# Down projections of the middle feed-forward groups in blocks of seven products

## The chip, the cores and the metric

The kernel runs on one core of a Trainium2 chip. Its time is the device time of one execution in microseconds. Five engines work beside each other and wait for one another by semaphores: TensorE (PE, matmuls; PEld is its loading of the stationary operand), VectorE (DVE), ScalarE (ACT), GpSimd (POOL) and SyncE (SP), which issues most transfers. Matmuls write to PSUM, which has eight banks of 128 x 512 fp32; all other tiles are in SBUF.

## What is computed

A model of two layers on 512 tokens of width 1024: each layer has a mixing part and a feed-forward part, each between two RMS norms and added to the residual `h`. The change concerns the feed-forward part alone:

```python
f = rmsnorm(h, ln_ffn_pre[layer])
f = (jax.nn.silu(f @ w_ffn_gate[layer]) * (f @ w_ffn_up[layer])) @ w_ffn_down[layer]
h = h + rmsnorm(f, ln_ffn_post[layer])
```

All is fp32. The inner width is 2816, which is 22 inner tiles of 128.

## The kernel before

**Three products for one.** To keep fp32 accuracy every operand is split into a high part, rounded to the matmul's type fp32r, and the low rest. `split` (line 239) makes both: ACT casts (`hi`), DVE subtracts (`lo`). `mm3` (lines 191 to 193) multiplies high by high, high by low and low by high, so each 128 x 128 block costs three matmuls. Weights are loaded by SP into `raw` tiles (128 x 1024, four buffers) and split into `whi`/`wlo` tiles (128 x 512, eight buffers each). Split activations lie in a pool of 36 tiles.

**The feed-forward part** (`feed_forward`, line 1150). The inner tiles 0 and 1 come first, apart from the rest; the others go in the groups of line 1154. For each group, gate and up are computed for two inner tiles at a time, then the group's hidden rows are multiplied by the down weights.

*Gate and up* (`Seven`, line 1018). For two inner tiles the product with `f` is a 2 x 2 block product (two inner tiles by two halves of 256 tokens each, and two halves of the width 1024) made with seven block products instead of eight, Strassen's way. One block product is 4 x 3 = 12 matmuls with the weights stationary and 256 tokens moving. `sums` makes the four sums of weights on DVE, `parts` splits a weight block, `run` makes one product, `carry` copies a PSUM tile with ACT so that later products can accumulate on it. The PSUM tiles are `x`, `p` and `q`. `end` makes the rows, by `gate_rows` (line 1169) or `up_rows` (line 1176): gate rows are scaled and passed through Silu, up rows are multiplied by them, which gives the hidden row `u` of one inner tile (128 x 512 tokens); line 1181 splits it into `fs`. The first pair of a layer runs as `FirstSeven`, with its gate and up products interleaved.

*Down* (lines 1231 to 1240). For each half `dh` of the output width, four PSUM tiles (one per block of 128 tokens, tags `mm` and `lg`) collect over all inner tiles of the group; here the hidden tokens are stationary and 512 output columns of the weights move. `down_weights` loads two inner tiles at a time (512 KB) and splits them. At the end DVE adds each PSUM tile to the running sum `ys[tb][dh]` in SBUF (line 1240).

The last group (18, 22) is handed to `tail_of` and is worked on with the norm that follows.

**Order.** The program is written down in one order, and a scheduler places each engine's instructions by that order as priority, taking a later one where an earlier one isn't ready in its own estimate. On the chip each engine then keeps its fixed order. A tile is taken from its pool when a buffer is free. `behind` and `high_priority` shift single pieces.

Of the kernel before, what the change touches and what calls it, by code (L numbers as in the profile page):

```python
# [15 lines left out]
P = 128  # L16
# [24 lines left out]
def hybrid(ctx: ExitStack, tc: tile.TileContext, i: dict, out: bass.AP):  # L41
# [26 lines left out]
    def temp(s, shape=(P, T), tag="t", bufs=4, dt=F32):  # L68
        return tp.tile(list(shape), dt, tag=tag, name=name(s), bufs=bufs)
# [4 lines left out]
    def ps(tag, shape=(P, T), s="ps"):  # L74
        return pp.tile(list(shape), F32, tag=tag, name=name(s), bufs=2 if tag == "tr" else 3)
# [55 lines left out]
    def pair_of_parts(n=512, aside=False):  # L131
        if aside:
            return act("whi"), act("wlo")
        return (wp.tile([P, max(n, 512)], F32R, tag="hi", name=name("whi"), bufs=8)[:, :n],
                wp.tile([P, max(n, 512)], F32R, tag="lo", name=name("wlo"), bufs=8)[:, :n])
# [44 lines left out]
    def down_weights(layer, k, dh, aside=False):  # L180
        return moving_pair(i["w_down"][layer, 4 * dh : 4 * dh + 4, :, k : k + 2, :]
                           .rearrange("m p k c -> p m (k c)"), aside)

    def token_products(o, x, w, tb, start, stop):

        c = slice(tb * P, (tb + 1) * P)
        return mm3(o.rearrange("p (m c) -> p m c", c=P), (x[0][:, c], x[1][:, c]), w, start, stop)
# [50 lines left out]
    def split(src, hi, lo, eng=None):  # L238
        last_parts[:] = A.copy(hi, src), (eng or V).tensor_sub(lo, src, hi)  # L239
# [22 lines left out]
    class Norm:  # L262


        def __init__(self, width=T):
            self.r4 = small("r4")
            self.acc, self.width = None, width
# [66 lines left out]
    def parts(s):  # L334
        return [(act(f"{s}hi"), act(f"{s}lo")) for _ in range(KT)]
# [682 lines left out]
    class Seven:  # L1018
# [28 lines left out]
        def product(self, o, w, n, more=False):  # L1047
            for k, w in enumerate(cut(w, P)):
                mm3(o, w, self.xs[n][k], k == 0 and not more, k == KT // 2 - 1, more)
# [100 lines left out]
    def feed_forward(layer, phase, xp, meanwhile=None):  # L1150

        nnorm = PairNorm()
        rb = rbc
        groups = ((2, 8), (8, 14), (14, 18), (18, 22))

        def hidden(gate, up, f, cols):
            c0, c1 = cols
            n = c1 - c0
            gr = temp("gr")
            V.tensor_mul(gr[:, :n], gate, rb[:, c0:c1])  # L1160
            s = temp("silu")
            A.activation(s[:, :n], gr[:, :n], AF.Silu)
            ff = temp("f")
            V.tensor_mul(ff[:, :n], up, s[:, :n])
            split(ff[:, :n], f[0][:, c0:c1], f[1][:, c0:c1])

        gates = [None] * 3

        def gate_rows(row, src, g):

            end = V.tensor_mul(g, src, rb)
            gates[2] = A.activation(g, g, AF.Silu, scale=-1.0 if row else 1.0)
            gates[row] = g
            return end

        def up_rows(row, src, u, fs):
            if row:
                end = V.scalar_tensor_tensor(out=u, in0=src, scalar=-1.0, in1=gates[1], op0=ALU.mult, op1=ALU.mult)
            else:
                end = V.tensor_mul(u, src, gates[0])  # L1180
            split(u, *fs[len(fs) - 2 + row])
            return end

        fs = [(act("fhi"), act("flo")) for _ in range(2)]

        def first(n, aside):
            return prepared(i["w_up" if n % 2 else "w_gate"][layer, n // 2], (KT, P), aside)

        def evac_first(outs, cols):
            for m in range(2):  # L1190
                hidden(outs[2 * m], outs[2 * m + 1], fs[m], cols)

        scaled = {}
        a, close = boundary(phase, G_MIX_POST + layer, G_FFN_PRE + layer, nnorm, rb, first, evac_first, scaled)
        w = [down_weights(layer, 0, dh) for dh in range(2)]
        close()
        xs, last = combined(a, scaled, xp)
        last()
        ys = [[plain("y") for _ in range(2)] for _ in range(TB)]
        for tb in range(TB):  # L1200
            for dh in range(2):
                o = ps("lg" if dh else "mm", s="y")
                for k in range(2):
                    token_products(o, fs[k], w[dh][k], tb, k == 0, k == 1)
                A.copy(ys[tb][dh], o)

        for gi, (k0, k1) in enumerate(groups):
            fs = []
            for m in range(k0, k1, 2):
                if meanwhile and m == k1 - 2 and gi == len(groups) - 1:  # L1210
                    next(meanwhile)
                fs += [(act("fhi"), act("flo")) for _ in range(2)]
                Kind = FirstSeven if m == 2 else Seven
                sevens((lambda: Kind(xs, lambda n: i["w_gate"][layer, m + n], gate_rows),
                        lambda: Kind(xs, lambda n: i["w_up"][layer, m + n],
                                     lambda row, src, t: up_rows(row, src, t, fs))), m == 2, m == k0)
            nk = k1 - k0
            if gi == len(groups) - 1:
                if layer:
                    with behind([gates[2]]):  # L1220
                        A.preload_act_table_set("natural_log_exp_and_others")
                if meanwhile:
                    next(meanwhile)

                eps = small("eps")
                V.tensor_mul(eps, nnorm.r4, nnorm.r4)
                V.reciprocal(eps, eps)
                V.tensor_scalar_mul(eps, eps, RMS_EPS)
                return tail_of(fs, lambda kp, dh, aside, k0=k0: down_weights(layer, k0 + 2 * kp, dh, aside), ys, eps,
                               layer == 1)  # L1230
            for dh in range(2):
                outs = [ps("mm" if tb < 2 else "lg", s="y") for tb in range(TB)]
                for kp in range(nk // 2):
                    w = down_weights(layer, k0 + 2 * kp, dh)
                    for x in range(2):
                        k = 2 * kp + x
                        for tb in range(TB):
                            token_products(outs[tb], fs[k], w[x], tb, k == 0, k == nk - 1)
                for tb in range(TB):
                    V.tensor_add(ys[tb][dh], outs[tb], ys[tb][dh])  # L1240


    def layer_b(phase, fp):
# [297 lines left out]
```

## Time and profile before

| | us |
|---|---|
| median of 3 runs | 1105.83 |
| lowest, highest | 1105.72, 1106.42 |
| the profiled execution | 1106.21 |
| its span, first to last instruction | 1104.1 |

The profile is of one execution. In its rows a line number is that of the helper that issued an instruction, so tiles tell parts apart: `x`, `a` (written as `p` above) and `e` (`q`) are PSUM tiles of gate and up, `y` those of down. Rows of the timeline give start, duration, engine, line, operation and tiles; in brackets stands the idle time ahead of an instruction and what ended it. A window row gives a stretch from start to end, its length, and the busy time and number of rows of each engine.

### The profile page before, as it was taken

To read this page: it belongs to the slowest core of one execution; us is meant where nothing else is said; L and a number is where in the kernel's file an instruction comes from. 1 tells how busy PE (TensorE), PEld (TensorE's weight loads), DVE (VectorE), ACT (ScalarE), POOL (GpSimd) and SP (SyncE) were. 2 spreads that over 40 slices of the span, in tenths; PEclk is the share of its full clock that TensorE was granted. 3 is DMA by queue.
4 is the path that set the end of the run, shared out by engine and by line. 5 is a ranking of instruction groups with operands and counts; after the bars stand their busy time and mean duration, and the time that the engine had idled before them with its cause. 6 is when DMAs were issued, how large, how long until landed. Compare 5 with 4: busy or idle time off the path is not lost.

```text
span 1104.1 us, 19424 instructions
## 1 busy us (share of the span) xinstructions
PE 1096.2 (99%) x7363; PEld 1001.4 (91%) x7363; DVE 870.0 (79%) x1714; ACT 683.5 (62%) x1428; POOL 24.3 (2%) x40
## 2 busy tenths in 40 slices
PE   9999999999999999999999999999999999999998
PEld 7998889999899899998988998889999899899996
DVE  7879759996697497796968789868996698587775
ACT  7776578664366264477747788878664266254464
POOL 0000000000000000001000000000000000000000
PEclk9999999999999999999999999999999999999999
DMA  7521331334134133255222554531234134233232
GB/s 268 161 80 54 119 115 39 115 115 134 58 115 138 58 111 115 77 157 171 74 79 63 156 133 121 145 115 39 77 111 138 58 114 132 61 110 120 77 96 77
DMA packets 64020, 118.64 MB, mean 107 GB/s; under 512 B 5236, under 2 KB 40072, under 8 KB 63928
## 3 DMA queue, kind: packets, MB, share of 16 engines
q1 hardware_dynamic: 63032, 116.57, 34.9%
q8 instruction: 58, 0.95, 0.4%
q0 software_dynamic: 192, 0.52, 0.2%
q10 hardware_dynamic: 704, 0.32, 0.1%
q14 instruction: 34, 0.28, 0.1%
HBM read 105.23 MB, written 2.10 MB: 97 GB/s over the span
## 4 chain that ended last, share of the span: by engine, by line
PE 94%; DVE 3%; ACT 2%; issue 1%; DMA 0%; SPq 0%; DVEq 0%; ACTq 0%
PE y L191 10%; PE y L193 10%; PE y L192 10%; PE a L192 5%; PE a L193 5%; PE a L191 5%; PE ps L191 4%; PE ps L193 4%; PE ps L192 4%; PE x L191 3%; PE x L192 3%; PE x L193 3%; PE e L191 3%; PE e L192 3%; PE e L193 3%; PE v L191 2%
## 5 line engine op out<-in xcount | busy, mean ns | idle before, releaser
L239 ACT CAST whi<-raw 128x512 fp32r<-128x512 f32 x460 | 278.2, 619 | 265.2 <-PE y L193 119.5
L239 DVE TENSOR_TENSOR wlo<-raw,whi 128x512 fp32r<-128x512 f32 x460 | 310.4, 688 | 128.6 <-ACT whi L239 125.2
L191 PE MATMUL y<-whi,fhi 128*128 128x512 f32 (+1 forms) x356 | 139.8, 393 | 0.0
L193 PE MATMUL y<-whi,flo 128*128 128x512 f32 (+1 forms) x356 | 139.2, 392 | 0.0
L192 PE MATMUL y<-wlo,fhi 128*128 128x512 f32 (+1 forms) x356 | 138.9, 390 | 0.0
L191 PE MATMUL x<-xshi,whi 128*128 128x256 f32 x320 | 90.1, 281 | 0.2
L191 PE MATMUL a<-xshi,whi 128*128 128x256 f32 x320 | 89.9, 281 | 0.0
L192 PE MATMUL a<-xslo,whi 128*128 128x256 f32 x320 | 89.8, 281 | 0.0
L192 PE MATMUL x<-xslo,whi 128*128 128x256 f32 x320 | 89.8, 281 | 0.0
L193 PE MATMUL a<-xshi,wlo 128*128 128x256 f32 x320 | 89.8, 280 | 0.0
L193 PE MATMUL x<-xshi,wlo 128*128 128x256 f32 x320 | 89.7, 280 | 0.0
L193 PEld LDWEIGHTS y<-whi,flo 128*128 128x128 f32 x356 | 66.8, 188 | 15.5 <-DVE flo L239 0.2
L192 PEld LDWEIGHTS y<-wlo,fhi 128*128 128x128 f32 x356 | 66.9, 188 | 15.0 <-DVE wlo L239 0.2
L191 PEld LDWEIGHTS y<-whi,fhi 128*128 128x128 f32 x356 | 66.9, 188 | 14.7 <-ACT fhi L239 0.3
L191 PE MATMUL ps<-xshi,whi 128*128 128x256 f32 (+1 forms) x224 | 68.4, 305 | 0.0
L192 PE MATMUL ps<-xslo,whi 128*128 128x256 f32 (+1 forms) x224 | 66.6, 298 | 0.0
L193 PE MATMUL ps<-xshi,wlo 128*128 128x256 f32 (+1 forms) x224 | 66.3, 297 | 0.0
L191 PEld LDWEIGHTS x<-xshi,whi 128*128 128x128 f32 x320 | 60.2, 188 | 0.6 <-ACT x L1055 0.6
L192 PEld LDWEIGHTS a<-xslo,whi 128*128 128x128 f32 x320 | 60.2, 188 | 0.3
L191 PEld LDWEIGHTS a<-xshi,whi 128*128 128x128 f32 x320 | 60.2, 188 | 0.3
L193 PEld LDWEIGHTS a<-xshi,wlo 128*128 128x128 f32 x320 | 60.3, 188 | 0.0
L193 PEld LDWEIGHTS x<-xshi,wlo 128*128 128x128 f32 x320 | 60.3, 188 | 0.0
(310 smaller groups left out, 3056.1 us busy)
## 6 DMA issues: line engine op xcount, KB each, us to landing
raw<-in_w_gate SPq DMA_DIRECT2D x44, 512.0 KB, 3.5
raw<-in_w_up SPq DMA_DIRECT2D x44, 512.0 KB, 3.5
raw<-in_w_down SPq DMA_DIRECT2D x44, 512.0 KB, 3.9
raw<-in_w_out SPq DMA_DIRECT2D x16, 512.0 KB, 3.7
raw<-in_w_b_q SPq DMA_DIRECT2D x8, 512.0 KB, 4.5
raw<-in_w_a_v SPq DMA_DIRECT2D x6, 512.0 KB, 7.8
raw<-in_w_a_u SPq DMA_DIRECT2D x6, 512.0 KB
raw<-in_w_v SPq DMA_DIRECT2D x6, 512.0 KB, 3.5
```

The costliest lines, as they stand in the source:

```text
L191: PE.matmul(o, w[0], x[0], start=start, stop=False, skip_group_check=more)
L192: PE.matmul(o, w[0], x[1], start=False, stop=False, skip_group_check=more)
L193: return PE.matmul(o, w[1], x[0], start=False, stop=stop, skip_group_check=more)
L239: last_parts[:] = A.copy(hi, src), (eng or V).tensor_sub(lo, src, hi)
```

## The change

The groups are now (2, 6), (6, 10), (10, 14), (14, 18) and (18, 22). For all but the last, the down product of two inner tiles is itself a 2 x 2 block product: two inner tiles, two halves of the tokens (256 each) and the two halves of the output width. It is made with seven products instead of eight.

`Inner` takes the two hidden rows `u0` and `u1` of a pair and makes the seven left operands: the left half of `u0` (`first`), `u1` whole (two operands), and two tiles of differences and sums (`both`, `other`, two operands each), all split. For the first pair of a group (`aside`) the low parts of the last two are made otherwise: ACT writes the negative of the high part, and a DMA issued by POOL adds the source to it. `DownSeven` loads both halves of a pair's down weights, makes four sums on DVE and splits seven blocks. `product` multiplies one of them with two blocks of 128 tokens, 6 matmuls of 512 columns. `down_sevens` runs the products of both pairs of a group, a and b, in an order that shares PSUM tiles between outputs; it holds eight. Of the outputs, some are copied to SBUF by ACT and added to one or two `ys` tiles by accumulating DMAs from POOL (`put`), others are added by DVE (`final`). Gate and up, `carry` among them, stay as they were.

```diff
-        groups = ((2, 8), (8, 14), (14, 18), (18, 22))
+        groups = ((2, 6), (6, 10), (10, 14), (14, 18), (18, 22))
...
-            split(u, *fs[len(fs) - 2 + row])
+            if done:
+                done(row, u)
+            else:
+                split(u, *fs[len(fs) - 2 + row])
...
+        def split_aside(src, hi, lo, aside):
+            if not aside:
+                return split(src, hi, lo)
+            A.copy(hi, src)
+            A.activation(lo, hi, AF.Copy, scale=-1.0)
+            G.dma_start(lo, src, accum_op=ALU.add)
...
+            def combine(self, u0, u1):
+                left, right = (slice(*c) for c in HALVES)
+                first = tp.tile([P, 2, 256], F32R, tag="acc", name=name("b11"), bufs=2)
+                split(u0[:, left], first[:, 0, :], first[:, 1, :])
+                second, both, other = [(act("fhi"), act("flo")) for _ in range(3)]
+                split(u1, *second)
+                V.tensor_sub(u0[:, left], u0[:, right], u0[:, left])
+                V.tensor_sub(u0[:, right], u1[:, right], u0[:, right])
+                V.tensor_sub(u1[:, right], u0[:, left], u1[:, right])
+                V.tensor_add(u1[:, left], u1[:, right], u1[:, left])
+                split_aside(u0, *both, self.aside)
+                split_aside(u1, *other, self.aside)
+                half = lambda pair, c: tuple(t[:, c] for t in pair)
+                self.x = {1: (first[:, 0, :], first[:, 1, :]), 2: half(second, left), 3: half(second, right),
+                          4: half(other, left), 5: half(both, left), 6: half(other, right), 7: half(both, right)}
...
+        class DownSeven:
...
+                a11, a12, a21, a22 = (r[:, :, x, :] for r in raws for x in range(2))
+                self.w = {4: a22}
+                s3 = temp("s3").rearrange("p (m c) -> p m c", m=4)
+                V.tensor_sub(s3, a11, a21)
+                self.w[1] = self.parts(a11)
+                V.tensor_add(a21, a21, a22)
+                self.w[2] = self.parts(a12)
+                V.tensor_sub(a11, a11, a21)
+                V.tensor_add(a12, a11, a12)
+                self.w.update({3: a12, 5: a21, 6: a11, 7: s3})
...
+            def product(self, outs, n, start, stop):
+                w = self.w[n]
+                if n > 2:
+                    w = self.parts(w)
+                for x, o in enumerate(outs):
+                    c = slice(x * P, (x + 1) * P)
+                    mm3(o, tuple(t[:, c] for t in self.x[n]), w, start, stop, True)
+
+        def down_sevens(pairs):
+
+            def put(x, *where):
+                some = prob("yo")
+                A.copy(some, x)
+                for tb, dh in where:
+                    G.dma_start(ys[tb][dh], some, accum_op=ALU.add)
+
+            def final(x, tb, dh):
+                V.tensor_add(ys[tb][dh], x, ys[tb][dh])
+
+            a, b = DownSeven(pairs[0]), None
+            chain = [ps("lg", s="yc") for _ in range(2)]
+            a.product(chain, 1, True, False)
+            lows = [ps("mm", s="yl") for _ in range(2)]
+            a.product(lows, 2, True, False)
+            shared = [ps(t, s="ys") for t in ("tr", "tr")]
+            a.product(shared, 7, True, False)
+            ups = [ps(t, s="yu") for t in ("mm", "lg")]
+            a.product(ups, 3, True, False)
+            b = DownSeven(pairs[1])
+            b.product(chain, 1, False, True)
+            for x in range(2):
+                put(chain[x], (x, 0))
+            b.product(shared, 7, False, True)
+            for x in range(2):
+                put(shared[x], (x, 1), (x + 2, 1))
+            for u in (a, b):
+                u.product(chain, 6, False, u is b)
+            for x in range(2):
+                A.copy(shared[x], chain[x])
+            b.product(ups, 3, False, True)
+            for x in range(2):
+                final(ups[x], x + 2, 0)
+            a.product(chain, 5, False, False)
+            a.product(shared, 4, False, False)
+            b.product(lows, 2, False, True)
+            for x in range(2):
+                final(lows[x], x, 0)
+            b.product(chain, 5, False, True)
+            for x in range(2):
+                put(chain[x], (x + 2, 0), (x + 2, 1))
+            b.product(shared, 4, False, True)
+            for x in range(2):
+                final(shared[x], x, 1)
...
+                if gi < len(groups) - 1:
+                    pairs.append(Inner(m, m < k1 - 2))
...
-            for dh in range(2):
-                outs = [ps("mm" if tb < 2 else "lg", s="y") for tb in range(TB)]
...
-                for tb in range(TB):
-                    V.tensor_add(ys[tb][dh], outs[tb], ys[tb][dh])
+            down_sevens(pairs)
```

More of the change, by code (lines that the diff above doesn't have):

```diff
@@ L1174, in gate_rows, with up_rows @@
             return end
-        def up_rows(row, src, u, fs):
+        def up_rows(row, src, u, fs, done):
             if row:
@@ new lines, in feed_forward, with __init__, __call__ @@
+        class Inner:
+            def __init__(self, k, aside):
+                self.k, self.aside, self.u = k, aside, {}
+            def __call__(self, row, u):
+                self.u[row] = u
+                if len(self.u) == 2:
+                    self.combine(self.u[0], self.u[1])
+            def combine(self, u0, u1):
[13 more added lines that the diff above has]
+                          4: half(other, left), 5: half(both, left), 6: half(other, right), 7: half(both, right)}
@@ new lines, in feed_forward, with __init__, parts @@
+        class DownSeven:
+            def __init__(self, pair):
+                self.x = pair.x
+                raws = []
+                for dh in range(2):
+                    raw = wp.tile([P, 1024], F32, tag="raw", name=name("raw"), bufs=4)
+                    last_load[0] = nc.sync.dma_start(
+                        raw.rearrange("p (m c) -> p m c", m=4),
+                        i["w_down"][layer, 4 * dh : 4 * dh + 4, :, pair.k : pair.k + 2, :].rearrange("m p k c -> p m (k c)"))
+                    raws.append(raw.rearrange("p (m k c) -> p m k c", m=4, k=2))
+                a11, a12, a21, a22 = (r[:, :, x, :] for r in raws for x in range(2))
[8 more added lines that the diff above has]
+                self.w.update({3: a12, 5: a21, 6: a11, 7: s3})
+            def parts(self, src):
+                pair = pair_of_parts()
+                split(src, *(t.rearrange("p (m c) -> p m c", m=4) for t in pair))
+                return pair
+            def product(self, outs, n, start, stop):
[5 more added lines that the diff above has]
+                    mm3(o, tuple(t[:, c] for t in self.x[n]), w, start, stop, True)
@@ L1207, in feed_forward @@
         for gi, (k0, k1) in enumerate(groups):
-            fs = []
+            fs, pairs = [], []
             for m in range(k0, k1, 2):
@@ L1211, in feed_forward @@
                     next(meanwhile)
-                fs += [(act("fhi"), act("flo")) for _ in range(2)]
+                if gi < len(groups) - 1:
+                    pairs.append(Inner(m, m < k1 - 2))
+                else:
+                    fs += [(act("fhi"), act("flo")) for _ in range(2)]
                 Kind = FirstSeven if m == 2 else Seven
@@ L1215, in feed_forward @@
                         lambda: Kind(xs, lambda n: i["w_up"][layer, m + n],
-                                     lambda row, src, t: up_rows(row, src, t, fs))), m == 2, m == k0)
+                                     lambda row, src, t: up_rows(row, src, t, fs, pairs and pairs[-1]))), m == 2, m == k0)
             nk = k1 - k0
@@ L1230, in feed_forward @@
                                layer == 1)
-            for dh in range(2):
-                outs = [ps("mm" if tb < 2 else "lg", s="y") for tb in range(TB)]
[L1233 to L1236, printed above, removed]
-                        for tb in range(TB):
-                            token_products(outs[tb], fs[k], w[x], tb, k == 0, k == nk - 1)
-                for tb in range(TB):
-                    V.tensor_add(ys[tb][dh], outs[tb], ys[tb][dh])
+            down_sevens(pairs)
     def layer_b(phase, fp):
```

## The prediction

> **What bounds the kernel now.** I read the page first, for the shares of the engines.
>
> ```profile
> span 1104.1 us, 19424 instructions
> ## 1 busy us (share of the span) xinstructions
> PE 1096.2 (99%) x7363; PEld 1001.4 (91%) x7363; DVE 870.0 (79%) x1714; ACT 683.5 (62%) x1428; POOL 24.3 (2%) x40
> ```
>
> PE is never without work, but a busy PE may be a slow PE, so I then cut the feed-forward stage into its alternating parts with the view that sums engines over windows. The windows are, for layer 0, gate and up of a group, its down block, and so on through the three groups that are changed; then those three groups as a whole for each layer; last, one stretch early in layer 1.
>
> ```profile
> core 0: us, PE busy (x) PEld busy (x) DVE busy (x) ACT busy (x) POOL busy (x), PEclk, DMA share, GB/s
> 202.22:262.33 60.11, 60.07 (x505) 59.85 (x504) 54.24 (x98) 39.97 (x82) 0.00 (x0) 1.00 0.41 124
> 262.33:295.74 33.41, 33.41 (x147) 27.03 (x145) 17.84 (x30) 8.61 (x14) 0.00 (x0) 1.00 0.26 79
> 295.74:355.34 59.60, 59.60 (x505) 59.60 (x504) 52.04 (x89) 38.12 (x76) 0.00 (x0) 1.00 0.39 116
> 355.34:388.75 33.41, 33.41 (x146) 27.05 (x145) 17.81 (x30) 8.61 (x14) 0.00 (x0) 1.00 0.25 78
> 388.75:428.53 39.78, 39.78 (x337) 39.77 (x336) 33.29 (x58) 24.99 (x50) 0.00 (x0) 1.00 0.41 121
> 428.53:450.80 22.27, 22.27 (x98) 18.03 (x97) 15.12 (x25) 6.11 (x10) 0.00 (x0) 1.00 0.22 69
> 202.22:450.80 248.58, 248.54 (x1729) 231.32 (x1728) 190.35 (x322) 126.42 (x246) 0.00 (x0) 1.00 0.35 105
> 784.12:1032.13 248.01, 247.89 (x1730) 230.66 (x1728) 190.14 (x322) 126.66 (x246) 0.00 (x0) 1.00 0.35 105
> 797.00:835.00 38.00, 37.88 (x320) 37.48 (x319) 37.97 (x69) 25.08 (x51) 0.00 (x0) 1.00 0.32 102
> ```
>
> The step from one matmul to the next is what counts, and the code gives their number: 504 matmuls of 256 columns in 59.60 us is 0.118 us each; 144 of 512 columns in 33.41 us is 0.232, and 96 in 22.27 us is 0.232 again. The steps are the same in every part and the clock is full, so there is no waiting in these stretches: **PE is the bound, by the number of its matmuls.** A removed 512-column matmul is worth 0.232 us.
>
> DVE is the second engine: 190.35 of 248.58 us (77%), unevenly: about 90% beside gate and up, 53% to 68% beside the down blocks. From 797 to 835 it is full (37.97 of 38.00). What it costs when it is pressed is read from starts that follow each other:
>
> ```profile
> 428.44 0.68 DVE L1178 SCALAR_TENSOR_TENSOR s<-s,s 128x512 f32<-128x512 f32 x1
> 429.04 0.68 DVE L1180 TENSOR_TENSOR s<-x,s 128x512 f32<-128x512 f32 x1
> 429.64 0.68 DVE L239 TENSOR_TENSOR wlo<-raw,whi 128x512 fp32r<-128x512 f32 x1
> ...
> 805.77 0.42 DVE L1117 TENSOR_TENSOR s<-e,s 128x256 f32<-128x256 f32 x1
> 806.11 0.42 DVE L1118 TENSOR_TENSOR s<-a,s 128x256 f32<-128x256 f32 x1
> ```
>
> Rows overlap: a 512-wide one takes 0.60 us of the engine, a 256-wide one 0.34.
>
> Last, what DVE and ACT wait for while PE is in a down block (timeline, then costliest groups by form).
>
> ```profile
> 428.62 0.62 ACT L239 CAST whi<-raw 128x512 fp32r<-128x512 f32 x1 [0.81 <-PE x L192]
> ...
> 434.30 0.62 ACT L239 CAST whi<-raw 128x512 fp32r<-128x512 f32 x1 [2.16 <-PE y L193]
> 437.08 0.62 ACT L239 CAST whi<-s 128x512 fp32r<-128x512 f32 x1 [2.16 <-PE y L193]
> ```
> ```profile
> L239 ACT CAST whi<-raw 128x512 fp32r<-128x512 f32 x460 | 278.2, 619 | 265.2 <-PE y L193 119.5 <-PE a L192 38.8 <-PE x L192 37.8
> ...
> L1240 DVE TENSOR_TENSOR y<-y,y 128x512 f32<-128x512 f32 x48 | 29.7, 682 | 0.0
> L1205 ACT COPY y<-y 128x512 f32<-128x512 f32 x16 | 9.4, 588 | 8.4 <-PE y L193 8.1
> ```
>
> Each cast of a weight half waits for PE to finish with an older one: all eight hi/lo buffers are full, so the preparation stands about seven products ahead of PE at the end of a gate/up part. That lead is what the change will draw on.
>
> **The change, part by part.**
>
> PE. Per pair of inner tiles the direct product takes 2 tiles x 4 token blocks x 2 halves x 3 = 48 matmuls; seven products over two token blocks take 7 x 2 x 3 = 42. Eight pairs a layer, two layers: 96 matmuls fewer, 96 x 0.232 = **22.3 us**. Gate and up keep their matmuls. The cut into four groups instead of three adds one passage per layer from up to down, which costs nothing in the rows above (no part is longer than its matmuls).
>
> DVE, per layer. Weights: 7 splits instead of 4 per pair and 4 sums, +7 rows x 8 pairs x 0.60 = 33.6 us. Hidden rows: a pair set aside (four a layer) has 0.34 + 0.60 + 4 x 0.34 = 2.30 in place of two splits at 1.20, +1.10; the other four also split two more tiles, 3.50, +2.30; together 13.6. Output: before, 24 additions a layer (half of the x48 of L1240), after 4 groups x 6 = 24, so nothing. Sum **+47.2 us**. All of it is hidden by PE as long as DVE fits: PE's new time per layer is 248.3 - 11.1 = 237.2. DVE's by busy time is 190.2 + 47.2 = 237.4 (100%); but busy counts 0.68 where the engine is free after 0.60, and by the steps the 322 rows, 32 of them 256 wide, are 290 x 0.60 + 32 x 0.34 = 184.9, with the change 232.1 (98%). So the cover is nearly used up: five microseconds a layer are left, and every wait of DVE beyond them is paid by PE.
>
> ACT, per layer: 24 weight casts x 0.62 = 14.9; hidden rows, four aside pairs with four more 512-wide copies at most, 4 x 2.3, and four others 4 x 1.0, some 13; eight PSUM copies a group x 0.59 = 18.9. In all +47 on 126.4, 173 of 237 (73%): it fits.
>
> POOL and DMA, per layer: ten accumulating transfers of 256 KB a group and two per aside pair, 48. The kernel before has no accumulating DMA; the nearest is the plain copy between partitions that POOL issues.
>
> ```profile
> raw<-in_w_down SPq DMA_DIRECT2D x44, 512.0 KB, 3.9
> ...
> memk<-memk POOLq DMA_DIRECT2D x4, 128.0 KB, 4.6
> ```
>
> A copy of 128 KB lands 4.6 us after its issue. For 256 KB with a read of the target I take 6 us, between 4.6 and twice that, 9.2. What waits for them is DVE's last additions: `lows` are added five products (7 us) after the chain's first copy is sent, and `shared` eight products (11 us) after its. So 6 us are hidden, and 9.2 would hold DVE back for some 2 us in a block, which the lead of seven products covers once.
>
> SP. The down weights are still 16 loads of 512 KB a layer, but a pair's two halves are needed together, and the first tile is released late (its last split, for product 4, is the twelfth of fourteen). By eight buffers and 1.39 us a product this split is done about 6.5 us into the block, the next gate's second load lands 3.9 us later, and the gate starts at 19.5: hidden.
>
> PSUM. The block holds all eight banks. The last two that it takes are the old up block's: `q`, free after the addition at L1083, and `x`, free after row 0's multiplication, 0.6 us after the last matmul; they are needed 2.8 and 4.2 us in. The copies of `chain` must end before product 6 writes on it, 1.4 us after: two copies of 0.59 just fit.
>
> The passage from up to down. From the last up matmul PE has four products of the older pair, 24 x 0.232 = 5.6 us, then product 1 and, at 7.0 us, product 7 of the younger pair. DVE needs by then 0.60 (row 0), 0.34 + 0.60 (b11, u1), 4 x 0.34 and 0.60: 3.5 us, and about 1 us of ACT copies between, 4.5 in all. That holds if both pairs' weight sums are made earlier, in the lead, as the rows at 428 show for the weights now. I take a stall of 0.5 us for six of the eight blocks.
>
> The first group of each layer is different, as DVE is full there. The chain of waits of layer 1 ends:
>
> ```profile
> 811.33 0.61 DVE raw L1044
> 811.95 0.02 issue
> 811.97 0.62 ACT whi L239
> 812.59 0.28 ACT x L1055
> 812.87 0.04 issue
> 812.91 0.38 PE x L191
> ```
>
> A DVE that is late holds ACT's cast, behind which ACT's PSUM copy is queued, for which PE waits. The aside pair's extra 1.10 us falls just ahead of this; I take 1.1 us there plus 0.4 for the first down block, 1.5 a layer.
>
> Sum: 22.3 - 6 x 0.5 - 2 x 1.5 = 16.3 us. The profiled execution took 1106.21 us with its span of 1104.1; 1106.2 - 16.3 = 1089.9, and as the median lies 0.4 us under that execution, **1089.5 us**. Without any stall it is 1083.5.
>
> **The rivals.** DVE becomes the bound. For: 98% by its steps, and outside full stretches it does wait for ACT. Against: from 797 to 835 it ran without a hole. Does it lose 5% to waits, its work is 232.1 x 1.05 = 243.7 a layer, 6.5 over PE's 237.2: the gain is 22.3 - 13.0 = 9.3, 1096.5 us. At 7% nothing is left.
>
> Slower: the passage from up to down is not prepared. If the younger pair's weights come behind the hidden rows on DVE, then from the last up matmul stand 4.1 us of hidden rows (both other splits with them), 3.6 of the older pair's sums and first splits, 1.2 for its products 7 and 3, 3.6 of the younger pair's and 0.6 for its product 7: 13.1 us against PE's 7.0. 6.1 us in each of eight blocks is 49 us, less 22.3: 1132 us. It decides from a stall of 22.3 / 8 = 2.8 us a block on. For: the hidden rows come first in the program, and raw tiles are four, all held by the two pairs. Against: the full buffers at 428, which show weights made before the hidden rows exist.
>
> The transfers come late. The Trainium skill, SBUF — State Buffer, section Who interferes with whom, has POOL unable to write the descriptors of its DMAs while VectorE is in a two-port mode, and says that tensor_tensor has no such mode. In this kernel's terms: DVE's addition of `lows` stands at the head of its queue until the transfer lands, and PE runs on for the seven prepared products, 10 us; it needs landings over 7 + 10 = 17 us. With 20 us each block would lose 3 us, 24 in all: 1107, no difference. The row of 4.6 us, issued while DVE was at work, does not point that way; I give it 0.02.
>
> No change in matmuls is not a rival: the count is in the code.
>
> **How the numbers follow.** About 0.2%, 2.2 us, is what a measurement of this kernel can tell. Forecast (1083 to 1095): 0.62. DVE bound in part (1095 to 1103.6): 0.14. Within 0.2%: 0.07, of it 0.05 by DVE at 7% and 0.02 by the transfers. Slower, by the passage or by DVE losing more: 0.17. Faster 0.76, same 0.07, slower 0.17. Eight in ten: from 1083, no stall at all, to 1104, nearly all of the DVE case.
>
> **What would show it.** Down blocks of 84 matmuls and 19.5 us with a step of 0.232 show the first term. DVE near 97% in the changed windows with PE steps of 0.118 beside gate and up show that the cover holds; PE gaps inside gate and up, with DVE full, show the DVE rival; a gap of PE ahead of the younger pair's products 1 or 7, released by DVE, shows the passage; DVE additions to `ys` that idle for a DMA show late transfers. I am wrong if the sum of gaps in the eight blocks is over 12 us, or if DVE's rows grow longer beside POOL's transfers.

## The result and the profile after

| | us |
|---|---|
| before, median of 4 runs | 1105.89 (1105.72 to 1106.42) |
| after, median of 4 runs | 1124.61 (1122.06 to 1125.12) |
| after / before | 1.0164, 95% interval 1.0146 to 1.0181 |
| predicted | 1089.5, range 1083 to 1104 |

The change makes the kernel 18.7 us slower; the prediction had it 16.3 us faster. The page of the kernel after first; of its queues (third part) the columns are packets, MB and the time of the packets as a share of 16 engines' span, of its transfers (last part) the size and the median time from issue to landing.

```profile
span 1123.4 us, 19912 instructions
## 1 busy us (share of the span) xinstructions
PE 1091.1 (97%) x7267; PEld 995.8 (89%) x7267; DVE 956.2 (85%) x1906; ACT 760.7 (68%) x1588; POOL 107.7 (10%) x136
...
q1 hardware_dynamic: 63032, 116.57, 33.6%
q0 software_dynamic: 14016, 25.70, 13.3%
...
y<-yo POOLq DMA_DIRECT2D x80, 256.0 KB, 8.1
```

PE has its 96 matmuls fewer (7363 before), yet its share fell from 99% to 97%: it now stands idle for some 32 us, against 8 before. DVE grew by 86.2 us and ACT by 77.2. Queue q0, which POOL issues, moved 0.52 MB before (0.2% of the sixteen DMA engines' time); now it moves 25.70 MB, nearly all of it accumulating transfers, and takes 13.3%: per MB 1.8 times what the loads of q1 take (13.3 / 25.70 against 33.6 / 116.57).

Where the time goes is read from the windows, cut as before: gate and up of a group, its down block, and so on. The columns are those of the same view in the prediction (busy time and rows of PE, PEld, DVE, ACT and POOL, granted clock, DMA share, GB/s). Layer 0 is the upper half to 498.28, layer 1 the rest.

```profile
203.64:244.02 40.38, 40.38 (x337) 40.03 (x336) 37.30 (x71) 27.90 (x60) 1.93 (x2) 1.00 0.42 118
244.02:264.15 20.13, 19.73 (x86) 15.66 (x85) 16.52 (x31) 11.78 (x23) 5.21 (x6) 1.00 0.57 138
264.15:307.71 43.56, 41.54 (x337) 41.36 (x336) 42.68 (x77) 29.02 (x59) 5.20 (x6) 0.96 0.59 155
307.71:327.22 19.51, 19.51 (x87) 15.79 (x85) 16.35 (x30) 11.10 (x21) 5.29 (x6) 1.00 0.61 156
327.22:370.78 43.56, 41.04 (x338) 40.11 (x336) 42.17 (x76) 29.34 (x60) 5.21 (x6) 1.00 0.61 149
...
390.25:435.06 44.81, 41.82 (x338) 41.44 (x337) 39.26 (x71) 26.82 (x54) 4.33 (x5) 0.96 0.55 137
...
454.55:498.28 43.73, 40.64 (x338) 40.05 (x336) 37.96 (x69) 27.62 (x58) 2.61 (x3) 1.00 0.56 153
791.78:832.00 40.22, 40.22 (x337) 40.02 (x336) 36.28 (x69) 27.84 (x59) 1.80 (x2) 1.00 0.42 119
832.00:853.32 21.32, 19.81 (x86) 15.68 (x85) 17.00 (x31) 11.40 (x22) 5.20 (x6) 1.00 0.53 123
853.32:896.42 43.10, 40.49 (x337) 39.89 (x336) 42.70 (x77) 29.41 (x60) 5.16 (x6) 1.00 0.61 160
...
915.94:959.49 43.55, 41.45 (x338) 41.27 (x337) 43.05 (x77) 29.91 (x60) 5.15 (x6) 0.96 0.62 151
...
978.96:1026.41 47.45, 43.28 (x337) 42.70 (x336) 39.54 (x71) 26.86 (x54) 4.27 (x5) 0.93 0.53 130
...
1045.87:1091.51 45.64, 42.04 (x337) 41.44 (x336) 33.91 (x58) 24.33 (x49) 2.58 (x3) 0.96 0.48 134
```

The down blocks (84 matmuls) are what was forecast: 19.5 us with PE busy throughout, and 20.13 and 21.32 for the first one of each layer. All the rest is lost *behind* a block: 336 matmuls at 0.1183 us are 39.75 us, and the eight gate/up parts that follow a block take 43.1 to 47.45, together 355.4 against 318.0, **37.4 us**. With 2.4 in the two first blocks (beyond 19.5) and 1.1 in the two first gate/up parts that is 41 us, against the 22.3 saved: 18.7 us slower. (In four of these parts DVE is busy for 97% or more of the window, 42.68 of 43.56 us in the first, which looks like the DVE rival of the prediction. The experiments say otherwise.)

What happens behind a block is seen best around 390. The same view in windows of 2 us, some left out:

```profile
384.00:386.00 2.00, 2.00 (x10) 1.66 (x9) 2.00 (x4) 0.74 (x2) 0.00 (x0) 1.00 1.13 208
...
392.00:394.00 2.00, 0.11 (x1) 0.14 (x2) 1.55 (x3) 0.71 (x2) 0.35 (x1) 1.00 1.08 254
...
396.00:398.00 2.00, 2.00 (x11) 2.00 (x10) 2.00 (x5) 0.62 (x2) 0.00 (x0) 0.50 1.13 229
...
400.00:402.00 2.00, 2.00 (x20) 2.00 (x19) 0.00 (x0) 1.20 (x3) 0.00 (x0) 1.00 0.22 64
```

From 380 to 398 all sixteen DMA engines are busy (nine windows with shares from 1.01 to 1.13). In this stretch lie POOL's transfers and, from SP's timeline, the next part's loads (start, duration of both issues, engine, line):

```profile
379.72 3.04 SPq L144 DMA_DIRECT2D raw<-in_w_up  x2
```

What waits for these loads is shown by DVE's timeline, then PE's.

```profile
392.45 0.69 DVE L1040 TENSOR_TENSOR s<-raw,raw 128x512 f32<-128x512 f32 x1 [2.11 <-DMA raw<-in_w_up]
393.06 1.28 DVE L1265 TENSOR_TENSOR y<-ys,y 128x512 f32<-128x512 f32 x2
```
```profile
391.57 0.28 PE L193 MATMUL a<-xshi,wlo 128*128 128x256 f32 x1
393.89 0.36 PE L191 MATMUL e<-t3hi,whi 128*128 128x256 f32 x1 [2.04 <-DVE y L1265]
...
395.03 0.41 PE L191 MATMUL e<-t3hi,whi 128*128 128x256 f32 x1
395.23 0.42 PE L192 MATMUL e<-t3lo,whi 128*128 128x256 f32 x1
```

The loads were issued by 382.76 and are used at 392.45, 9.7 us later. DVE stood idle for 2.1 us with the sum of weights of the next `Seven` (L1040, which needs both raw tiles) at the head of its queue. **Behind it stood the down block's last additions** (L1265, `y<-ys`), which free the PSUM bank into which PE's product writes `e`. So PE waited 2.04 us for an addition that stood behind a wait for a load. Then comes a second price: a microsecond after the gap the step of PE is 0.20 us (395.03 to 395.23) and no longer 0.118, and the granted clock of the window from 396 to 398 is 0.50. Over the whole profiled execution the mean granted clock fell from 0.999 to 0.989, an estimated 11 of the 1123 us at most.

The chain of waits in this stretch (start, duration, what) has a POOL transfer as its longest link, one into the `y` tile to which the addition adds. It landed at 392.56, just as the late load did, so here either alone would have held PE:

```profile
380.72 0.55 POOL y L1262
381.27 11.29 DMA y<-yo
...
393.06 0.70 DVE y L1265
...
393.89 0.36 PE e L191
```

This is one place. Over the whole run, the view of the line that issues these loads (L144) gives who waited for them (us, times) and their landing, after and, in the second fence, before; the third has PE's waits in the kernel after (waiter, what it waited for: us, times, longest).

```profile
  DVE s L1040: 36.2, 18
...
DMA to landing us min/median/max: 3.5/4.6/8.8
```
```profile
  DVE s L1040: 9.0, 8
...
DMA to landing us min/median/max: 3.4/3.5/5.1
```
```profile
PE a L191 <- ACT x L1055: 9.1, 4, 3.0
...
PE e L191 <- ACT whi L239: 6.7, 3, 2.6
...
PE e L191 <- DVE y L1265: 5.8, 5, 2.0
```

DVE's wait for weights in L1040 grew from 9.0 us to 36.2, and the median load lands in 4.6 us instead of 3.5. (The landing row doesn't hold every load: its largest is 8.8, and the one above took more.) PE then waits in three ways for what is queued behind L1040 on DVE: for DVE's additions; for ACT's cast (`whi`) of a later weight sum, which DVE makes behind L1040; or for ACT's PSUM copy (L1055), which stands behind a Silu (L1172) that waits for DVE's gate rows (L1171). Followed back in the chain view, the six longest of the waits of the second and third way (they end at 267.75, 857.48, 919.61, 471.12, 996.54 and 1062.92, 14.8 us together) come to an L1040 that had itself waited for its weights for 3.1 to 3.9 us.

### The profile page after: what moved, and what is told of

Read it like the earlier page. It is cut to its first block, busy times and chain, and to the rows that moved or that the text cites. A ratio compares the mean times of both kernels' runs of the same rounds, so it can differ in the third digit from the quotient of the medians.

```text
span 1123.4 us, 19912 instructions
## 1 busy us (share of the span) xinstructions
PE 1091.1 (97%) x7267; PEld 995.8 (89%) x7267; DVE 956.2 (85%) x1906; ACT 760.7 (68%) x1588; POOL 107.7 (10%) x136
## 3 DMA queue, kind: packets, MB, share of 16 engines
q1 hardware_dynamic: 63032, 116.57, 33.6%
q0 software_dynamic: 14016, 25.70, 13.3%
## 4 chain that ended last, share of the span: by engine, by line
PE 60%; DVE 18%; DMA 13%; issue 4%; ACT 4%; POOL 1%; DVEq 0%; SPq 0%; ACTq 0%
DVE wlo L239 6%; DMA raw<-in_w_gate 5%; PE y L191 4%; PE y L192 4%; PE y L193 4%; DMA y<-yo 4%; PE ps L191 4%; PE ps L193 4%; PE ps L192 4%; DMA raw<-in_w_down 3%; PE a L191 3%; PE a L193 2%; PE a L192 2%; PE v L191 2%; PE v L193 2%
## 5 line engine op out<-in xcount | busy, mean ns | idle before, releaser
L239 ACT CAST whi<-raw 128x512 fp32r<-128x512 f32 x492 | 293.1, 619 | 149.9 <-PE x L192 28.5
L239 DVE TENSOR_TENSOR wlo<-raw,whi 128x512 fp32r<-128x512 f32 x492 | 326.4, 684 | 30.9 <-ACT whi L239 29.3
L191 PE MATMUL a<-xshi,whi 128*128 128x256 f32 x320 | 90.8, 284 | 1.1 <-ACT e L1055 1.1
L191 PE MATMUL x<-xshi,whi 128*128 128x256 f32 x320 | 91.6, 286 | 0.3 <-ACT x L1055 0.3
L1262 POOL DMA_DIRECT2D y<-yo x80 | 69.6, 1263 | 210.9 <-ACT yo L1260 182.8
L191 PE MATMUL ps<-xshi,whi 128*128 128x256 f32 (+1 forms) x224 | 68.4, 305 | 0.0
L191 PEld LDWEIGHTS a<-xshi,whi 128*128 128x128 f32 x320 | 60.6, 189 | 2.6 <-ACT e L1055 2.2
L191 PEld LDWEIGHTS x<-xshi,whi 128*128 128x128 f32 x320 | 61.8, 193 | 1.0 <-ACT x L1055 0.9
L192 PEld LDWEIGHTS x<-xslo,whi 128*128 128x128 f32 x320 | 61.5, 192 | 0.0
L1040 DVE TENSOR_TENSOR s<-raw,raw 128x512 f32<-128x512 f32 x40 | 27.5, 688 | 36.4 <-DMA raw<-in_w_gate 32.4
L191 PE MATMUL e<-t3hi,whi 128*128 128x256 f32 x160 | 46.0, 287 | 12.5 <-ACT whi L239 6.7
L191 PE MATMUL a<-d2hi,whi 128*128 128x256 f32 x160 | 48.2, 302 | 9.1 <-ACT x L1055 9.1
L239 ACT CAST whi<-s 128x512 fp32r<-128x512 f32 x56 | 34.8, 621 | 31.1 <-DVE s L1040 16.2
```

Of the source, the lines that this page charges most:

```text
L191: PE.matmul(o, w[0], x[0], start=start, stop=False, skip_group_check=more)
L192: PE.matmul(o, w[0], x[1], start=False, stop=False, skip_group_check=more)
L1040: V.tensor_add(self.s3, a11, a21)
L1262: G.dma_start(ys[tb][dh], some, accum_op=ALU.add)
```

## The experiments

Three theories. **T1:** the accumulating transfers make the weight loads late. **T2:** DVE has too much work. **T3:** the order on DVE is at fault, a late load's consumer ahead of additions that could run. In the tables "wait" is DVE's at L1040 with its number, and the mean clock is the granted one, both of the profiled execution; ratios are to the kernel before on the same chip, with the 95% interval. Edits are to the kernel after unless said otherwise.

**Traffic and work, alone and together.** `e1_tiny_accum` keeps every instruction on every engine, but the accumulating transfers of the outputs move 16 of 128 partitions, so the other rows of those sums are left out. `e2_no_sums` leaves out the four sums of down weights, 64 DVE rows in all (1842 against 1906). `e9_tiny_no_sums` does both.

```diff
-                    G.dma_start(ys[tb][dh], some, accum_op=ALU.add)
+                    G.dma_start(ys[tb][dh][:16], some[:16], accum_op=ALU.add)
```
```diff
-                V.tensor_sub(s3, a11, a21)
...
-                V.tensor_add(a21, a21, a22)
...
-                V.tensor_sub(a11, a11, a21)
-                V.tensor_add(a12, a11, a12)
-                self.w.update({3: a12, 5: a21, 6: a11, 7: s3})
+                self.w.update({3: a12, 5: a21, 6: a11, 7: a21})
```

> The changed kernel, but each accumulating transfer into ys moves 16 of its 128 partitions (32 KB in place of 256 KB); the other 112 partitions of those outputs aren't added. Every engine's order is the same. Theory T1 (the accumulating transfers take the 16 DMA engines and delay the weight loads, up to 8.8 us in place of 3.5): the loads land in 3.5 to 4 us again, DVE's sums at L1040 wait under 10 us in all, and the time is 1083 to 1096 us. Theory T2 (DVE simply has too much to do: 956 us busy): the transfers don't matter, 1115 to 1125 us. Theory T3 (the order on DVE is the cause: a sum that waits for a load stands ahead of the additions that free PSUM): with loads in time this also falls to 1083 to 1096; finals_first tells it from T1.

> The changed kernel without the four sums of down weights in each DownSeven, so that five of the seven products use wrong operands: 32 DVE rows of 0.60 us fewer a layer, 38 us in all, transfers as before. T2: most of the loss is gone, 1085 to 1100 us. T1: the loads land as late as in the changed kernel and DVE still waits for them at L1040 for 25 us or more; 1108 to 1122 us.

> Small transfers (16 of 128 partitions) and no sums of down weights, together: part of the additions into ys left out and five products with wrong operands. What is left of the loss with small transfers alone (1097 us against 1083.5 without any wait): if it is DVE's work, it goes now, 1083 to 1089 us; if it is the order of the queues or the late loads that remain, it stays, 1093 to 1098 us.

| | median us | ratio | wait us |
|---|---|---|---|
| after | 1124.61 | 1.0164 [1.0146, 1.0181] | 36.2, 18 |
| e2, less work for DVE | 1123.75 | 1.0158 [1.0138, 1.0179] | 46.8, 26 |
| e1, small transfers | 1097.02 | 0.9915 [0.9898, 0.9931] | 14.3, 12 |
| e9, both | 1085.94 | 0.9814 [0.9797, 0.9831] | 10.4, 17 |

Taking the bytes away gains 27.6 us with DVE's work in place and 37.8 without it. Taking DVE's work away gains 0.9 us with the bytes in place, which is within the spread of the runs (1122.06 to 1125.12 for the kernel after), and 11.1 without them. So T2 alone is wrong and T1 comes first; DVE's missing slack is a second term that shows once the loads are in time. With both gone the time is 2.4 us from the 1083.5 that the prediction gave for no stall at all. (T1's ranges were missed by a little: e1 came out 1.0 us above its range, e2 1.8 us above.) The small transfers also come off the engines sooner, so e1 by itself does not tell what the bytes take from the loads from how late the transfers themselves are; but in the kernel after DVE's additions at L1265 waited for such a transfer for only 0.8 us in all, though a late one can hide behind L1040, as at 392.56.

Why less work for DVE gave nothing is seen in e2's rows. First SP's issue of the loads and DVE's use of them, then the DMA engines in the same stretch:

```profile
326.05 2.13 SPq L144 DMA_DIRECT2D raw<-in_w_gate  x2
...
331.36 0.68 DVE L239 TENSOR_TENSOR wlo<-raw,whi 128x512 fp32r<-128x512 f32 x1
335.93 0.69 DVE L1040 TENSOR_TENSOR s<-raw,raw 128x512 f32<-128x512 f32 x1 [3.89 <-DMA raw<-in_w_gate]
...
340.45 1.23 ACT L1172 ACTIVATE s<-s 128x512 f32<-128x512 f32 x2 [3.85 <-DVE s L1171]
341.58 0.37 ACT L1055 COPY x<-a 128x256 f32<-128x256 f32 x1
```
```profile
332.00:334.00 2.00, 2.00 (x20) 2.00 (x19) 0.04 (x1) 1.21 (x3) 0.00 (x0) 1.00 1.08 326
```

The loads were issued by 328.18, DVE had nothing else to do from 332.0 on, and they were there only at 335.9, 7.8 us after, with the DMA engines full. The stall is handed on: DVE's scaling of the gate rows (L1171) stands behind L1040, ACT's Silu (L1172) idles for it, and behind the Silu stands the PSUM copy (L1055) that PE waits for. A DVE that is quicker only waits longer. The same pair of loads in e9, where the transfers are small:

```profile
320.38 2.52 SPq L144 DMA_DIRECT2D raw<-in_w_gate  x2
...
327.11 0.69 DVE L1040 TENSOR_TENSOR s<-raw,raw 128x512 f32<-128x512 f32 x1 [0.33 <-DMA raw<-in_w_gate]
```

Issued by 322.90, used at 327.11: 4.2 us, not 7.8, after an issue of the same kind.

**The traffic in the kernel before.** `e6_before_traffic` adds ten accumulations of a tile of zeros (256 KB each) behind each of before's six down blocks; `e5_groups_only` gives it the new groups and nothing else.

```diff
+                nought = prob("nought")
+                G.memset(nought, 0.0)
+                for tb, half in [(tb, dh) for tb in range(TB)] + [(0, 0), (1, 0)] * dh:
+                    G.dma_start(ys[tb][half], nought, accum_op=ALU.add)
```

> The kernel before with ten accumulating transfers of zeros into ys (256 KB each) after each down block, issued by POOL, 60 in all; outputs unchanged. T1 in its plain form (the transfers delay the loads, and late loads stop PE): the loads land up to 6 to 9 us late and the time rises by 8 to 25 us. T1 with cover (late loads hurt only because DVE has no slack left and stands still behind them): the loads land as late, but DVE, 77% busy here, waits for them less and the time rises by under 5 us.

> The kernel before with only the new cut into groups (four tiles each), direct down products. All theories: the cut costs nothing by itself, within 3 us of the kernel before. If it costs 10 us or more, part of the loss is in the passages and not in the transfers.

The groups alone: 1106.12 us, 0.9995 [0.9985, 1.0004]; the further passage from up to down costs nothing, as predicted. The traffic alone: 1105.88 us, 0.9997 [0.9988, 1.0007], and a wait of 7.6 us in 8. The time is what the second form of T1 had, but not for its reason. Both forms took the loads to be late, and they were not: the loads of L144 land in 3.5 us at the median and 5.0 at most (3.5 and 5.1 in the kernel before). What the run shows is narrower: 60 such transfers cost nothing by themselves where loads and DVE have room. In the kernel after they meet loads that are needed at once.

**The order on DVE (T3).** `e3_finals_first` puts the weight sums of the second `Seven` behind the block's last addition.

```diff
-            for make in pair:
+            for n, make in enumerate(pair):
                 u = make()
-                with behind(ended if opens else ()):
+                with behind((closed if n else ended) if opens else ()):
                     u.sums()
-                opens = False
...
-                final(shared[x], x, 1)
+                closed[0] = final(shared[x], x, 1)
```

> The changed kernel with one edge more: in the first pair of a group the up block's sums (L1040) stand behind the last addition of the down block on DVE. Outputs unchanged. T3: the gaps of PE ahead of product 7 (two to three us in six groups) go and with them the slower clock behind them, 1085 to 1100 us. T1: those gaps go, 12 to 20 us of the loss with the clock, but the sums still wait for their loads and later gaps stay, 1104 to 1114 us. T2: no change over 5 us, 1118 to 1126 us.

1115.14 us, 1.0078 [1.0059, 1.0096]: 9.5 us of the loss is this order. The range for T1 ended at 1114. A wait of 29.2 us in 14 is left, so PE still waits, now mostly by way of ACT's casts and copies.

**Other ways to make the additions.** `e4_pool_adds` lets POOL add in SBUF in place of the ten transfers of a block. `e7_six_accums` reorders the products so that six transfers do, with two more DVE additions; `e8_six_accums_edge` adds e3's order to it. `e12_eight_edge` is e3 with eight transfers: chain's first output is added by DVE.

```diff
-                    G.dma_start(ys[tb][dh], some, accum_op=ALU.add)
+                    G.tensor_tensor(out=ys[tb][dh], in0=ys[tb][dh], in1=some, op=ALU.add)
```
```diff
-            ups = [ps(t, s="yu") for t in ("mm", "lg")]
-            a.product(ups, 3, True, False)
             b = DownSeven(pairs[1])
             b.product(chain, 1, False, True)
             for x in range(2):
-                put(chain[x], (x, 0))
+                final(chain[x], x, 0)
...
             b.product(shared, 4, False, True)
             for x in range(2):
                 final(shared[x], x, 1)
+            a.product(chain, 3, False, False)
+            b.product(chain, 3, False, True)
+            for x in range(2):
+                final(chain[x], x + 2, 0)
```

> The changed kernel with the ten accumulating transfers of a group replaced by ten additions on POOL, same sums, same order on PE and DVE. T1: as with the small transfers, 1083 to 1098 us, unless POOL's additions make DVE's rows longer (both then read two SBUF tiles): that would show as a mean of DVE's splits over 700 ns and a time over 1100 us. T2: 1115 us or more.

> The changed kernel with another order of the same products: the chain's first sum is added to ys by DVE from PSUM, and product 3 is collected on the chain after its copy is sent, so that six accumulating transfers a group are left of ten and the last two are sent 5.6 us before the block ends; DVE has two additions more a group. T1: less and earlier traffic, 1100 to 1114 us. T2 (DVE): 10 us of DVE work more in all, 1124 us or above.

> The same with the edge that puts the up block's sums behind the down block's last addition. T1: the remaining part of the loss that the edge takes from the changed kernel (9 us) shrinks with the traffic, 1096 to 1108 us.

> The changed kernel with the edge, four raw tiles, the same order of products, and the chain's first sum added to ys by DVE from PSUM: eight transfers a group in place of ten, 10 us of DVE work more in all. T1: the six transfers that meet the four loads become four, 1104 to 1112 us against 1115 with the edge alone. T2: 1118 us or above.

| | median us | ratio | wait us |
|---|---|---|---|
| e4 | 1160.82 | 1.0490 [1.0472, 1.0509] | 6.0, 6 |
| e7 | 1134.02 | 1.0245 [1.0230, 1.0261] | 1.5, 2 |
| e8 | 1134.41 | 1.0244 [1.0205, 1.0283] | 1.5, 2 |
| e12 | 1115.25 | 1.0070 [1.0047, 1.0093] | 20.9, 11 |

In e4 the loads are in time again (6.0 us), as T1 has it, and the kernel is the slowest of all. The costliest groups (busy us, mean ns of one):

```profile
L239 DVE TENSOR_TENSOR wlo<-raw,whi 128x512 fp32r<-128x512 f32 x492 | 376.1, 785 | 33.1 <-ACT whi L239 31.0
L1262 POOL TENSOR_TENSOR y<-y,yo 128x512 f32<-128x512 f32 x80 | 155.2, 1971 | 165.1 <-ACT yo L1260 165.0
```

A split on DVE takes 785 ns beside these additions and 684 in the kernel after, 50 us over 492 of them; in all DVE is busy for 64 us more (1020.5 against 956.2), and PE waits 34.4 us for its additions (`e` at L191 for L1265). The Trainium skill (SBUF — State Buffer, Who interferes with whom) says that a VectorE instruction with two SBUF inputs contends with a GpSimd instruction that reads SBUF; these two rows agree.

In e7 and e8 the expectation failed: less traffic, yet slower than the kernel after. e7's DVE and SP show a different lateness:

```profile
386.23 3.70 DVE L239 TENSOR_TENSOR wlo<-raw,whi 128x512 fp32r<-128x512 f32 x6
...
388.18 1.30 SPq L144 DMA_DIRECT2D raw<-in_w_gate  x2
...
394.58 1.29 DVE L239 TENSOR_TENSOR wlo<-raw,whi 128x512 fp32r<-128x512 f32 x2 [4.66 <-ACT whi L239]
```

The next part's loads are issued from 388.18 on, at the end of DVE's run of splits: the new order uses products 4 and 3 last, so by the code it holds every raw tile of both pairs to the end. DVE has nothing left at 389.93 and a hole of 4.66 us. Had the loads landed in 3.5 us it would still have waited: they are late by their *release* here. The wait has left L1040 for ACT's casts. In e12 the two transfers less gained nothing over e3: 1115.25 us, where T1 had 1104 to 1112.

**More raw tiles.** If loads are late because a tile is free too late for the slower transfer, a fifth raw tile must help though no byte of the traffic goes. `e13_raw5` has five raw tiles and, to make room, seven split pairs instead of eight; `e10_raw5_edge` adds e3's order; `e11_raw6_edge` has six and six; `e14_raw5_edge_tiny` is e10 with e1's small transfers (the same rows left out); `e15_raw5_eight_edge` is e10 with e12's eight transfers.

```diff
-        return (wp.tile([P, max(n, 512)], F32R, tag="hi", name=name("whi"), bufs=8)[:, :n],
-                wp.tile([P, max(n, 512)], F32R, tag="lo", name=name("wlo"), bufs=8)[:, :n])
+        return (wp.tile([P, max(n, 512)], F32R, tag="hi", name=name("whi"), bufs=7)[:, :n],
+                wp.tile([P, max(n, 512)], F32R, tag="lo", name=name("wlo"), bufs=7)[:, :n])
...
-        raw = wp.tile([P, 1024], F32, tag="raw", name=name("raw"), bufs=4)
+        raw = wp.tile([P, 1024], F32, tag="raw", name=name("raw"), bufs=5)
```

> The changed kernel with five raw weight tiles and seven split pairs, without the edge. If the fifth raw tile is what covers the late loads, 1100 to 1110 us, and the edge adds little beside it (against 1103.5 with both); if it works only with the edge, 1114 us or above.

> The changed kernel with the edge (up's sums behind the last down addition), five raw weight tiles in place of four, and seven split pairs in place of eight to make room. T1: a load is asked for earlier, so its lateness is covered; waits at L1040 fall under 15 us and the time is 1092 to 1106 us. If the lead of eight split pairs matters more than the loads, 1112 us or above.

> The same with six raw tiles and six split pairs. T1: waits at L1040 under 10 us, 1090 to 1104 us; if split pairs become short, above the kernel with five and seven.

> Five raw tiles, seven split pairs, the edge, and the accumulating transfers cut to 16 of 128 partitions (the other 112 of those outputs aren't added); every engine's order as in the kernel with full transfers. If five raw tiles cover the late loads, little is left for the transfers to cost: 1097 to 1103 us. If the transfers still cost what they did with four raw tiles (27 us), 1076 to 1084, which is under the matmuls alone and so can't be; in between, 1085 to 1096, the cover is in part.

> Five raw tiles, seven split pairs, the edge, and the chain's first sum added by DVE (eight transfers a group). If what is left is transfers that DVE's additions wait for (9.8 us in the profile of five raw tiles with the edge), 1096 to 1102 us; if DVE's work is the limit now, 10 us more of it give 1104 to 1114.

| | median us | ratio | wait us | mean clock |
|---|---|---|---|---|
| e13, 5 raw | 1104.81 | 0.9983 [0.9974, 0.9992] | 7.2, 10 | 0.999 |
| e10, 5 raw, order | 1103.46 | 0.9972 [0.9959, 0.9985] | 8.7, 10 | 0.999 |
| e11, 6 raw, order | 1119.25 | 1.0119 [1.0096, 1.0142] | 4.7, 2 | 0.994 |
| e14, e10 with small transfers | 1087.90 | 0.9836 [0.9820, 0.9852] | 7.2, 7 | 1.000 |
| e15, e10 with 8 transfers | 1098.94 | 0.9937 [0.9912, 0.9962] | 4.2, 5 | 0.994 |

One raw tile, with a split pair given up for it, takes away 19.8 us (1124.61 to 1104.81), with every byte of the traffic still there, and the wait is below that of the kernel before. What the order brings shrinks from 9.5 us to 1.4 (e13 to e10, within the spread of the runs), as it must if the order only hurts where loads are late. But the transfers are not free yet: e10 to e14 is 15.6 us. e10's waits say where, and e11's that it grows:

```profile
DVE y L1264 <- DMA y<-yo: 9.8, 7, 2.0
```
```profile
DVE y L1264 <- DMA y<-yo: 25.8, 11, 3.8
```

DVE's additions now wait for POOL's transfers into the same `ys` tiles. With loads in time these land last. In e11 the lead of prepared weights is six pairs instead of eight, and the same kind of wait is 25.8 us; the runs do not tell what the shorter lead costs from what this wait costs. Its range of 1090 to 1104 us was missed. e15 removes the transfers into the tiles to which `lows` is added and is the best version that computes all outputs: 7.0 us faster than before, 25.7 faster than after. Why it gains 4.5 us over e10 is not shown: all seven of e10's waits for a transfer stand at the other additions (`y<-ys`), and e15 still has 8.3 us of them in four. It is still 11 us from e14.

## Why the prediction was wrong

- **PE, right.** The blocks run at 0.232 us a matmul, 19.5 us each; 22.3 us were saved.
- **The passage from up to down, right, even cautious.** Six of eight blocks have no gap where 0.5 us was taken; the rival of an unprepared passage fell with them.
- **The first group, near.** 1.5 us a layer was taken; 1.3 in layer 0 (0.63 + 0.63) and 2.3 in layer 1 (0.47 + 1.82) were lost.
- **DVE's and ACT's amounts, near.** +86 us where 94 was worked out, and +77 where 94.
- **POOL and DMA, the step that failed.** "So 6 us are hidden" asked only who waits for the new transfers. It never asked what they take from others. Sixteen engines serve both queues; the accumulating one takes 13.3% of them, in bursts that begin within a block and run on behind it, where the engines are full for some 18 us in the place shown. And the landing of 6 us, at most 9.2, was short for these bursts: the median is 8.1 and the chain holds one of 11.29. e1 shows the size of the step: 27.6 us. (The seven microseconds ahead of the addition of `lows` were counted short as well: by the code seven products lie between, not five, and in the block shown the first copy of chain starts at 377.81 and that addition at 387.86. This made the forecast cautious and is not what failed.)
- **SP, wrong by the same omission.** That the next gate's second load "lands 3.9 us later" took a landing from a kernel whose DMA engines were a quarter to two fifths busy (0.22 to 0.41 in the windows of before). In the two places shown loads took 9.7 us (the kernel after) and 7.8 (e2). The release was about as forecast in the block from 370.78 on: its gate loads were issued by 377.28, 6.5 us into the block. A fifth tile, with a split pair given up for it, is worth 19.8 us.
- **"The cover is nearly used up", right, and not followed up.** The prediction said that every wait of DVE beyond five microseconds a layer is paid by PE and then looked for such waits only in DVE's own rows. They came from the loads. The rival of a DVE-bound kernel fails as it was put: less work for DVE gained 0.9 us (e2), against 11.1 with small transfers.
- **The late-transfer rival named the wrong victim.** It asked for landings over 17 us and had DVE waiting for `y`; the longest transfer landed in 13.3 us, DVE's wait for them was 0.8 us in all, and what came late was a weight load, which needs only some 7 us to hurt. DVE's wait for `y` appears for real in e10 and e11. The rows do not point to the rival's mechanism, POOL kept from its issues by DVE: an issue takes 1.26 us on average, a landing 8.1 at the median, so most of the time passes after the issue.
- **A missing term.** No gap was taken to cost more than its length. Some cost half a clock for 3 to 4 us afterwards, by the estimate above up to 11 us in sum.

Of the signs that the text named for being wrong, gaps of over 12 us in the blocks and longer DVE rows, neither came: the gaps lie behind the blocks. There the text had taken PE gaps with DVE full for a sign of the DVE rival, and in four of the eight parts that sign came, although less DVE work by itself gained only 0.9 us.

Not settled: how the 36 us of waiting at L1040 divide between engines shared with the transfers and tiles released late. At 390 in the kernel after and at 328 in e2 it is sharing, since the loads were issued in time for their former landing; in e7 it is release. A fifth tile may help against either.

## What to carry to other kernels

A transfer that nobody waits for still takes the DMA engines from the loads that somebody does wait for: price its bytes against the busiest stretch of the windows' DMA share, not against its own consumer. When a change uses up the slack of the second engine, look at every load that engine waits for, and at what stands behind that wait in its queue; a buffer more for the loads can be worth more than the work that was saved. And cut the parts *behind* a changed block as carefully as the block itself: here the block was just as forecast, and the loss lay after it.

## What the hardware showed beyond this

**A gap of 2 us can cost half the clock.** A microsecond after the gap of 2.04 us that ends at 393.89 the step is 0.20 us, with a granted clock of 0.50 in the window from 396 to 398. The Trainium skill (TensorE: Matmul & The Clock Gate, Part 1: The HAM clock gate) has the clock fall after an idle window of about 3.4 us, in a window that runs freely. This gap was shorter and the clock fell nevertheless; the windows from 454.55 and 853.32, in which the longest gaps are 2.41 and 2.58 us, keep a clock of 1.00. Here the measurement decides: gaps of this size are sometimes, not always, followed by the slow spell.

**An accumulating transfer lands late in a burst, not alone.** 256 KB land in 8.1 us (median) in the bursts of the kernel after and in 5.4 in those of e6, beside 3.6 for a plain load of 512 KB. The first two rows are e6's, the third is of the kernel after:

```profile
raw<-in_w_gate SPq DMA_DIRECT2D x44, 512.0 KB, 3.6
...
y<-nought POOLq DMA_DIRECT2D x60, 256.0 KB, 5.4
```
```profile
flo<-s POOLq DMA_DIRECT2D x16, 256.0 KB, 3.4
```

So in e6, where the kernel was not slowed, half the bytes took half as long again (5.4 against 3.6). But the sixteen accumulating transfers that make `flo` for the pairs set aside, of the same size and outside the bursts, land in 3.4 us. What the two kernels share is the engines' time: per MB 1.8 times that of the loads, in e6 (8.7% for 16.26 MB against 34.6% for 116.57) as in the kernel after.
